# Stick-breaking sums over the keys in float32r, with the softplus split in two parts

## The chip, the cores and the metric

The kernel runs on one core of a Trainium2 chip. The metric is the device time of one execution in microseconds (us). The engines of the core are named as in the profile: PE (TensorE, matrix products), PEld (its weight loads), DVE (VectorE), ACT (ScalarE), POOL (GpSimd) and SP, whose queue starts the transfers of the weights.

## The reference, cut to what matters

The program is a stack of layers over 256 tokens of width 1024: feed-forward, gated linear attention, feed-forward, feed-forward, **stick-breaking attention**, feed-forward, and then a second block with a mixture of experts. Only the stick-breaking layer is changed:

```python
z = einsum('bhtd,bhsd->bhts', q_blk, k) * scale          # 16 heads of 64
mask = s_pos[None, :] < t_pos[:, None]
sp = where(mask, softplus(z), 0.0)
rem = cumsum(sp, axis=3, reverse=True) - sp              # over the keys s, backwards
weights = where(mask, exp(log_sigmoid(z) - rem), 0.0)
o = einsum('bhts,bhsd->bhtd', weights, v)
```

Since log_sigmoid(z) is z - softplus(z), the exponent is z minus the sum of softplus over this key and all later ones that the query may see.

## The kernel before

All matrix products of the layers before the experts are made in float32r, in three terms: an operand x is cut into a part `hi` that float32r holds (an ACT Copy) and the rest `lo` (a DVE subtraction), and hi*hi + lo*hi + hi*lo is summed (`mm3`, L449 to L451). Weights come in tiles of 128x2048 (`raw`), which ACT and DVE cut into `whi` (L253) and `wlo` (L256) up to three tiles ahead of their use (`feed.ahead`). Nothing reorders the program: each engine's instructions stand in the order in which the code writes them.

The stick-breaking layer is `sb`. It takes the 16 heads in four groups `g` of four. For each group it projects queries (`proj_t`, 48 matmuls into `pj`), keys (the same) and values (`proj_v`, 48 matmuls into `pv`, L608 to L610). The attention of a group runs in three steps that are laid between the projections of the next group: `scores` after the next queries, `weights` after the next keys, `heads_out` after the next values. For the last group there are no further projections: `scores` follows its own values, and the output projection (`out_proj`, tiles `acco`) gives the cover instead, 36 matmuls between `scores` and `weights`, and 36 between `weights` and `heads_out`.

Each step does two halves `hc` (two heads each), half 0 first on every engine. A half holds the logits transposed (keys on the partitions), 384 columns for each head: 256 queries against the first 128 keys, and the last 128 queries against the last 128 keys. For a half

- `scores` makes the logits in plain f32 on PE (L870, L873), adds the mask with bf16 products (L876, L877), and then softplus(z) = max(z,0) + log(1+exp(-|z|)): Abs, Exp and Ln on ACT (L879 to L881, 128x768 each) and one DVE instruction (L882), into the tile `e`;
- `weights` subtracts the sums over the keys on PE, in plain f32: `ntri` (a triangle of -1) within a block of 128 keys (L887, L889), and `nones` (all -1) for what the second block adds to the queries of the first (L888). The trace shows every plain f32 matmul as two instructions. Then ACT takes Exp into `w` (L891);
- `heads_out` multiplies with the values (L899, L900) and cuts the result into `ohi` and `olo`.

Of the kernel before, what the change touches and what calls it, by code (L numbers as in the profile page):

```python
# [8 lines left out]
F32 = mybir.dt.float32  # L9
F32R = mybir.dt.float32r  # L10
# [3 lines left out]
AF = mybir.ActivationFunctionType  # L14
# [3 lines left out]
P = 128  # L18
T = 256
# [275 lines left out]
def body(ctx, tc, xin, small, cst, masks, groups, wts, out):  # L295
    nc = tc.nc
# [7 lines left out]
    mm = nc.tensor.matmul  # L304
# [30 lines left out]
    def C(name, a=0, b=None):  # L335
        o, w = coff[name]
        return ct[:, o + a:o + (w if b is None else b)]
# [3 lines left out]
    ident = C("ident")  # L341

    def bank(name):
        return psum.tile([P, 512], F32, name=name, tag="ps", bufs=4)
# [3 lines left out]
    def banks(name):  # L348

        return half2["pool"].tile([P, 2, 512], F32, name=name, tag="two", bufs=2)  # L350
# [6 lines left out]
    def tables(name):  # L357
        if in_place[0] != name:
            nc.scalar.preload_act_table_set(name)
        in_place[0] = name  # L360
# [59 lines left out]
    def stats_sums(ms=None):  # L420
        if ms is None:
            ms = bank("ms")
        held["ms"] = ms
        for tb in range(2):
            mm(ms[:, tb:tb + 1], lhsT=ssq[:, 0, tb * P:tb * P + P], rhs=one, start=True, stop=True)
        rsqrt(base, ms[:, 0:2], 2, 1.0 / D, "rs", rt)
# [158 lines left out]
    def proj_t(key, post=None, mid=None, first=False, ahead=None):  # L585

        hi, lo = feed.take(key)
        b = bank("pj")
        for s, c, opens in order(first):
            o = c * 256 + s * P  # L590
            mm3(b[:, s * T:(s + 1) * T], hi[:, o:o + P], lo[:, o:o + P], hhi[:, c, :], hlo[:, c, :], opens, c == ND - 1)
            if mid is not None and s == 0 and c == ND - 1:
                mid()
        if post is not None:
            post(b)
        feed.ahead(ahead)
        return b

    def proj_v(key, evac, mid=None, post=None):

        hi, lo = feed.take(key)
        b = bank("pv")
        for tb in range(2):
            ts = slice(tb * P, tb * P + P)
            o = b[:, tb * T:(tb + 1) * T]
            for c in range(ND):
                w = slice(c * 256, c * 256 + 256)
                mm(o, lhsT=hhi[:, c, ts], rhs=hi[:, w], start=(c == 0), stop=False)  # L608
                mm(o, lhsT=hhi[:, c, ts], rhs=lo[:, w], start=False, stop=False)
                mm(o, lhsT=hlo[:, c, ts], rhs=hi[:, w], start=False, stop=(c == ND - 1))  # L610
            if mid is not None and tb == 0:
                mid()
        for tb in range(2):
            evac(tb, b[:, tb * T:(tb + 1) * T])
        if post is not None:
            post()
        feed.ahead()
# [231 lines left out]
    def sb(gnext):  # L849
        with tc.tile_pool(name="sb", bufs=2) as pool, tc.tile_pool(name="sba", bufs=1, space=PS) as pacc:  # L850
            half2["pool"] = pacc
            ohi = pool.tile([P, ND, T], F32R, name="ohi", bufs=1)
            olo = pool.tile([P, ND, T], F32R, name="olo", bufs=1)
            cb = pool.tile([P, 2, P], BF16, name="cb", bufs=1)
            nones = pool.tile([P, P], F32, name="nones", bufs=1)
            nc.gpsimd.tensor_copy(cb[:, 0, :], ident)
            nc.gpsimd.tensor_copy(cb[:, 1, :], C("negs"))
            nc.gpsimd.memset(nones, -1.0)
            ntri = C("ntri")
            rb2 = rb[:, None, :].to_broadcast([P, 2, T])  # L860
            W3 = 3 * P
            def pair(b):
                return b.rearrange("p (s t) -> p s t", s=2)

            def scores(hc, qg, kg):

                z = banks("z")
                for k in range(2):
                    ps = slice(64 * k, 64 * k + 64)
                    mm(z[:, k, :T], lhsT=kg[ps, hc, :P], rhs=qg[ps, hc, :], start=True, stop=False, skip_group_check=True)  # L870
                for k in range(2):
                    ps = slice(64 * k, 64 * k + 64)
                    mm(z[:, k, T:W3], lhsT=kg[ps, hc, P:], rhs=qg[ps, hc, P:], start=False, stop=False,  # L873
                       skip_group_check=True)
                for k in range(2):
                    mm(z[:, k, :P], lhsT=cb[:, 0, :], rhs=cb[:, 1, :], start=False, stop=False, skip_group_check=True)  # L876
                    mm(z[:, k, T:W3], lhsT=cb[:, 0, :], rhs=cb[:, 1, :], start=False, stop=False, skip_group_check=True)  # L877
                e = pool.tile([P, 2, W3], F32, name="e", bufs=2)
                nc.scalar.activation(e, z[:, :, :W3], AF.Abs)  # L879
                nc.scalar.activation(e, e, AF.Exp, scale=-1.0)  # L880
                nc.scalar.activation(e, e, AF.Ln, bias=1.0)  # L881
                nc.vector.scalar_tensor_tensor(e, z[:, :, :W3], 0.0, e, op0=OP.max, op1=OP.add)  # L882
                return z, e

            def weights(z, e):
                for k in range(2):
                    mm(z[:, k, :T], lhsT=ntri, rhs=e[:, k, :T], start=False, stop=False, skip_group_check=True)  # L887
                    mm(z[:, k, P:T], lhsT=nones, rhs=e[:, k, T:], start=False, stop=False, skip_group_check=True)  # L888
                    mm(z[:, k, T:W3], lhsT=ntri, rhs=e[:, k, T:], start=False, stop=True, skip_group_check=True)  # L889
                w = pool.tile([P, 2, W3], F32, name="w", bufs=2)  # L890
                nc.scalar.activation(w, z[:, :, :W3], AF.Exp)  # L891
                return w

            def heads_out(n, hc, w, vg):
                o = bank("o")
                for k in range(2):
                    ps = slice(64 * k, 64 * k + 64)
                    vs = slice((2 * hc + k) * 64, (2 * hc + k) * 64 + 64)
                    mm(o[ps, :T], lhsT=vg[:, 0, vs], rhs=w[:, k, :T], start=True, stop=False)  # L899
                    mm(o[ps, P:T], lhsT=vg[:, 1, vs], rhs=w[:, k, T:], start=False, stop=True)  # L900
                nc.scalar.activation(ohi[:, n, :], o[:, :T], AF.Copy)
                nc.vector.tensor_sub(olo[:, n, :], o[:, :T], ohi[:, n, :].bitcast(F32))

            def attention(g, qg, kg, vg):
                ze = [scores(hc, qg, kg) for hc in range(2)]
                yield
                ws = [weights(*x) for x in ze]
                yield
                for hc in range(2):
                    heads_out(2 * g + hc, hc, ws[hc], vg)  # L910
                yield

            steps = iter(())
            tables(EXPLN)
            for g in range(4):
                qg = pool.tile([P, 2, T], F32, name="qg")
                kg = pool.tile([P, 2, T], F32, name="kg")
                vg = pool.tile([P, 2, T], F32, name="vg")

                def q_out(b):  # L920
                    nc.vector.scalar_tensor_tensor(qg, pair(b), 0.125, rb2, op0=OP.mult, op1=OP.mult)

                bq = proj_t(("col", "sb_w_in", 0, g * 256), post=q_out if g else lambda b: stats_sums(), first=g == 0)
                next(steps, None)

                def k_out(b):
                    if not g:
                        q_out(bq)
                    nc.vector.tensor_mul(kg, pair(b), rb2)

                proj_t(("col", "sb_w_in", 0, 1024 + g * 256), post=k_out, mid=stats_spread if g == 0 else None)
                next(steps, None)
                proj_v(("col", "sb_w_in", 0, 2048 + g * 256), lambda tb, b: nc.scalar.activation(
                    vg[:, tb, :], b, AF.Copy, scale=rt[:, tb:tb + 1]))
                next(steps, None)
                steps = attention(g, qg, kg, vg)
            next(steps, None)
            out_proj("sb_w_out", lambda c: (ohi[:, c, :], olo[:, c, :]), gnext, early=list(range(6)), mid=steps)
# [694 lines left out]
    ffn("ffn2", 0, g_ffn1[:, 8:16])  # L1633
    ffn("ffn1", 1, g_mix[:, 8:16])
    sb(g_ffn2[:, 8:16])
    late = ctx.enter_context(tc.tile_pool(name="late", bufs=1))
    g12 = late.tile([P, ND], F32, name="g12")
# [58 lines left out]
```

## Time and profile before

| | |
|---|---|
| time, 3 runs | 1588.01, 1588.44, 1591.41 us; median 1588.44 |
| profiled execution | 1587.87 us, of which its span (first to last instruction) is 1585.5 us |
| PE busy in the span | 1431.3 us, 90% |
| DVE, ACT busy | 781.4 us (49%), 569.1 us (36%) |
| the chain that ended last | PE 68%, DMA 23%, DVE 5%, ACT 3% |
| where `sb` lies | its projections run from about 679 to 770 us, its output projection to about 800 us |

Busy shares are means over the whole span; the stage that is changed is some 8% of it. What counts there is which engine the others wait for, and that is read from the stage itself.

### The profile page before, as it was taken

The numbers are of one execution on the slowest core, as the hardware profiler recorded it, in microseconds if no ns is written. First come the engines' busy times: TensorE is split into PE (matmuls) and PEld (weight loads), VectorE is DVE, ScalarE is ACT, GpSimd is POOL, SyncE is SP. The second block draws the span as 40 slices with busy tenths as digits, with TensorE's granted clock in tenths as the row PEclk, the third lists the DMA queues.
The fourth block names the chain that finished last, engine by engine and source line by source line (L and its number), as shares of the span: only waits on it lengthen the run. The fifth ranks groups of instructions, "written<-read, shape, count | busy, mean of one in ns | idle before, by whom it ended". The sixth has DMA issues, their size and how long they took to land.

```text
span 1585.5 us, 31150 instructions
## 1 busy us (share of the span) xinstructions
PE 1431.3 (90%) x13785; PEld 1249.2 (79%) x13785; DVE 781.4 (49%) x1163; ACT 569.1 (36%) x708; POOL 52.8 (3%) x53
## 2 busy tenths in 40 slices
PE   8999999999999999999999999999996666676665
PEld 7999999999999999999999999989752233232222
DVE  6755677776667666673376556776320010010001
ACT  5444455454444544464554444444210000000000
POOL 0000014100000000000010000100000000000000
PEclk9999999999999999999999999999899888788887
DMA  7655544246554555443345555427899999999997
GB/s 291 236 189 187 186 144 166 98 171 229 200 184 159 224 192 213 185 161 127 114 160 213 187 187 186 162 81 318 342 420 420 421 421 419 421 421 420 421 420 286
DMA packets 56474, 395.60 MB, mean 250 GB/s; under 512 B 6400, under 2 KB 6656, under 8 KB 8976
## 3 DMA queue, kind: packets, MB, share of 16 engines
q1 hardware_dynamic: 56336, 393.57, 63.9%
q8 instruction: 110, 1.80, 0.4%
q14 instruction: 28, 0.23, 0.0%
HBM read 392.50 MB, written 1.05 MB: 248 GB/s over the span
## 4 chain that ended last, share of the span: by engine, by line
PE 68%; DMA 23%; DVE 5%; ACT 3%; issue 1%; SPq 0%; ACTq 0%
PE gu L451 10%; PE gu L449 10%; PE gu L450 10%; DMA raw<-wts 7%; DMA whi<-wts 6%; PE acc L451 5%; PE acc L449 5%; PE acc L450 5%; DMA sX<-wts 4%; PE pj L449 3%; DMA sF<-wts 3%; PE pj L450 3%; PE pj L451 3%; DMA h<-wts 2%; PE gx L1492 2%; DVE wlo L256 1%
## 5 line engine op out<-in xcount | busy, mean ns | idle before, releaser
L256 DVE TENSOR_TENSOR wlo<-raw,whi 128x2048 fp32r<-128x2048 f32 (+1 forms) x186 | 413.0, 2231 | 200.0 <-ACT whi L253 200.0
L449 PE MATMUL gu<-hhi,whi 128*128 128x256 f32 x1408 | 394.8, 280 | 7.3 <-ACT whi L253 7.3
L451 PE MATMUL gu<-hhi,wlo 128*128 128x256 f32 x1408 | 394.3, 280 | 1.5 <-DVE wlo L256 1.5
L450 PE MATMUL gu<-hlo,whi 128*128 128x256 f32 x1408 | 394.0, 280 | 0.0
L253 ACT ACTIVATE whi<-raw 128x2048 fp32r<-128x2048 f32 (+1 forms) x186 | 341.9, 1851 | 45.1 <-issue 34.8
L449 PEld LDWEIGHTS gu<-hhi,whi 128*128 128x128 f32 x1408 | 266.5, 189 | 7.3 <-ACT whi L253 7.3
L451 PEld LDWEIGHTS gu<-hhi,wlo 128*128 128x128 f32 x1408 | 267.5, 190 | 2.1 <-DVE wlo L256 2.1
L450 PEld LDWEIGHTS gu<-hlo,whi 128*128 128x128 f32 x1408 | 268.0, 190 | 0.2 <-DVE hlo L400 0.2
L449 PE MATMUL acc<-ahi,whi 128*128 128x256 f32 x704 | 196.0, 278 | 0.0
L450 PE MATMUL acc<-alo,whi 128*128 128x256 f32 x704 | 196.0, 278 | 0.0
L451 PE MATMUL acc<-ahi,wlo 128*128 128x256 f32 x704 | 196.0, 278 | 0.0
L1531 DVE TENSOR_SCALAR gp<-ptb,ct 128x256 f32<-128x256 f32 x32 | 15.5, 483 | 281.7 <-PE ptb L1529 281.7
L1498 ACT ACTIVATE gp<-gx 128x256 f32<-128x256 f32 x32 | 12.3, 383 | 393.7 <-PE gx L1492 393.7
L489 ACT ACTIVATE sg<-gp 128x256 f32<-128x256 f32 x88 | 36.8, 418 | 290.9 <-DVE gp L488 280.6
L450 PEld LDWEIGHTS acc<-alo,whi 128*128 128x128 f32 x704 | 132.9, 189 | 0.0
L451 PEld LDWEIGHTS acc<-ahi,wlo 128*128 128x128 f32 x704 | 132.8, 189 | 0.0
L449 PEld LDWEIGHTS acc<-ahi,whi 128*128 128x128 f32 x704 | 132.1, 188 | 0.0
L449 PE MATMUL pj<-hhi,whi 128*128 128x256 f32 x416 | 118.4, 285 | 0.0
L450 PE MATMUL pj<-hlo,whi 128*128 128x256 f32 x416 | 116.7, 280 | 0.7 <-DVE hlo L400 0.7
L451 PE MATMUL pj<-hhi,wlo 128*128 128x256 f32 x416 | 116.5, 280 | 0.0
L450 PEld LDWEIGHTS pj<-hlo,whi 128*128 128x128 f32 x416 | 79.3, 191 | 0.9 <-DVE hlo L400 0.9
L449 PEld LDWEIGHTS pj<-hhi,whi 128*128 128x128 f32 x416 | 79.1, 190 | 1.0 <-issue 1.0
(438 smaller groups left out, 2007.3 us busy)
## 6 DMA issues: line engine op xcount, KB each, us to landing
raw<-wts SPq DMA_DIRECT2D x218, 1024.0 KB, 4.9
whi<-wts SPq DMA_DIRECT2D x37, 1024.0 KB, 19.8
wlo<-wts SPq DMA_DIRECT2D x37, 1024.0 KB, 19.8
sX<-wts SPq DMA_DIRECT2D x10, 1024.0 KB, 19.8
sA<-wts SPq DMA_DIRECT2D x10, 1024.0 KB, 19.8
sF<-wts SPq DMA_DIRECT2D x10, 1024.0 KB, 19.8
sG<-wts SPq DMA_DIRECT2D x10, 1024.0 KB, 19.8
sC<-wts SPq DMA_DIRECT2D x10, 1024.0 KB, 19.8
```

The costliest lines, as they stand in the source:

```text
L253: self.nc.scalar.activation(hi[:, o], r[:, o], AF.Copy)
L256: self.nc.vector.tensor_sub(lo[:, o], r[:, o], hi[:, o].bitcast(F32))
L449: mm(o, lhsT=whi, rhs=xhi, start=start, stop=False, skip_group_check=True)
L450: mm(o, lhsT=whi, rhs=xlo, start=False, stop=False, skip_group_check=True)
L451: mm(o, lhsT=wlo, rhs=xhi, start=False, stop=stop, skip_group_check=True)
L489: nc.scalar.activation(sg, gp, AF.Silu)
L1492: mm(b[rows[q], :W], lhsT=x[:, c, e % 8, :], rhs=w[:, o:o + W], start=(c == 0), stop=(c == ND - 1), skip_group_check=True)
L1498: nc.scalar.activation(s, b[:, :W], AF.Copy)
L1531: V.tensor_scalar(pt, b[:, :T], C("slot"), None, op0=OP.is_equal)
```

## The change

The sums over the keys are made in float32r. For this the softplus is split as the weights are: after DVE's L882 (now L889) ACT copies `e` into a float32r tile `hi` (L890), and DVE subtracts to get `lo` (L891). `weights` then makes four products for each head in place of three: `ntri` times 384 columns of `hi`, the same of `lo`, `nones` times 256 columns of `hi`, the same of `lo`. So that one product of 384 columns can take the place of two, the logits are laid out with the second key block first, and so that the `nones` product is 256 columns wide, `hi` and `lo` have 128 columns of zeros ahead of the data, which are written once at the start of `sb`. `ntri` and `nones` become float32r tiles that ACT writes, also at the start (L859, L860, L864). The two mask products of 128 columns become one of 256.

```diff
--- before.py
+++ after.py
@@ -852,11 +852,16 @@
             ohi = pool.tile([P, ND, T], F32R, name="ohi", bufs=1)
             olo = pool.tile([P, ND, T], F32R, name="olo", bufs=1)
             cb = pool.tile([P, 2, P], BF16, name="cb", bufs=1)
-            nones = pool.tile([P, P], F32, name="nones", bufs=1)
+            nones = pool.tile([P, P], F32R, name="nones", bufs=1)
+            ntri = pool.tile([P, P], F32R, name="ntri", bufs=1)
             nc.gpsimd.tensor_copy(cb[:, 0, :], ident)
             nc.gpsimd.tensor_copy(cb[:, 1, :], C("negs"))
-            nc.gpsimd.memset(nones, -1.0)
-            ntri = C("ntri")
+            nc.scalar.activation(ntri, C("ntri"), AF.Copy)
+            nc.scalar.activation(nones, ident, AF.Copy, scale=0.0, bias=-1.0)
+            es = [[pool.tile([P, 2, 512], F32R, name=f"e{n}{i}", bufs=1) for n in ("hi", "lo")] for i in range(2)]
+            for x in es:
+                for y in x:
+                    nc.scalar.activation(y[:, :, :P], cb, AF.Copy, scale=0.0)
             rb2 = rb[:, None, :].to_broadcast([P, 2, T])
             W3 = 3 * P
             def pair(b):
@@ -864,29 +869,34 @@
 
             def scores(hc, qg, kg):
 
+
                 z = banks("z")
                 for k in range(2):
                     ps = slice(64 * k, 64 * k + 64)
-                    mm(z[:, k, :T], lhsT=kg[ps, hc, :P], rhs=qg[ps, hc, :], start=True, stop=False, skip_group_check=True)
+                    mm(z[:, k, P:W3], lhsT=kg[ps, hc, :P], rhs=qg[ps, hc, :], start=True, stop=False, skip_group_check=True)
                 for k in range(2):
                     ps = slice(64 * k, 64 * k + 64)
-                    mm(z[:, k, T:W3], lhsT=kg[ps, hc, P:], rhs=qg[ps, hc, P:], start=False, stop=False,
+                    mm(z[:, k, :P], lhsT=kg[ps, hc, P:], rhs=qg[ps, hc, P:], start=False, stop=False,
                        skip_group_check=True)
                 for k in range(2):
-                    mm(z[:, k, :P], lhsT=cb[:, 0, :], rhs=cb[:, 1, :], start=False, stop=False, skip_group_check=True)
-                    mm(z[:, k, T:W3], lhsT=cb[:, 0, :], rhs=cb[:, 1, :], start=False, stop=False, skip_group_check=True)
+                    mm(z[:, k, :T], lhsT=cb[:, 0, :], rhs=cb[:, 1:2, :].to_broadcast([P, 2, P]), start=False, stop=False,
+                       skip_group_check=True)
                 e = pool.tile([P, 2, W3], F32, name="e", bufs=2)
+                hi, lo = (x[:, :, P:] for x in es[hc])
                 nc.scalar.activation(e, z[:, :, :W3], AF.Abs)
                 nc.scalar.activation(e, e, AF.Exp, scale=-1.0)
                 nc.scalar.activation(e, e, AF.Ln, bias=1.0)
                 nc.vector.scalar_tensor_tensor(e, z[:, :, :W3], 0.0, e, op0=OP.max, op1=OP.add)
-                return z, e
+                nc.scalar.activation(hi, e, AF.Copy)
+                nc.vector.tensor_sub(lo, e, hi.bitcast(F32))
+                return z, es[hc]
 
             def weights(z, e):
                 for k in range(2):
-                    mm(z[:, k, :T], lhsT=ntri, rhs=e[:, k, :T], start=False, stop=False, skip_group_check=True)
-                    mm(z[:, k, P:T], lhsT=nones, rhs=e[:, k, T:], start=False, stop=False, skip_group_check=True)
-                    mm(z[:, k, T:W3], lhsT=ntri, rhs=e[:, k, T:], start=False, stop=True, skip_group_check=True)
+                    for i, x in enumerate(e):
+                        mm(z[:, k, :W3], lhsT=ntri, rhs=x[:, k, P:], start=False, stop=False, skip_group_check=True)
+                    for i, x in enumerate(e):
+                        mm(z[:, k, P:W3], lhsT=nones, rhs=x[:, k, :T], start=False, stop=(i == 1), skip_group_check=True)
                 w = pool.tile([P, 2, W3], F32, name="w", bufs=2)
                 nc.scalar.activation(w, z[:, :, :W3], AF.Exp)
                 return w
@@ -896,8 +906,8 @@
                 for k in range(2):
                     ps = slice(64 * k, 64 * k + 64)
                     vs = slice((2 * hc + k) * 64, (2 * hc + k) * 64 + 64)
-                    mm(o[ps, :T], lhsT=vg[:, 0, vs], rhs=w[:, k, :T], start=True, stop=False)
-                    mm(o[ps, P:T], lhsT=vg[:, 1, vs], rhs=w[:, k, T:], start=False, stop=True)
+                    mm(o[ps, :T], lhsT=vg[:, 0, vs], rhs=w[:, k, P:], start=True, stop=False)
+                    mm(o[ps, P:T], lhsT=vg[:, 1, vs], rhs=w[:, k, :P], start=False, stop=True)
                 nc.scalar.activation(ohi[:, n, :], o[:, :T], AF.Copy)
                 nc.vector.tensor_sub(olo[:, n, :], o[:, :T], ohi[:, n, :].bitcast(F32))
```

On ACT, in a group's `scores`, the order of work was this (`e` is the softplus tile, `z` the logits; the last row is the cut of a weight tile that follows):

```order
L879 ACTIVATE e<-z 128x768
L880 ACTIVATE e<-e 128x768
L881 ACTIVATE e<-e 128x768
L879 ACTIVATE e<-z 128x768
L880 ACTIVATE e<-e 128x768
L881 ACTIVATE e<-e 128x768
L253 ACTIVATE whi<-raw 128x2048
```

and on ACT it is now this (`ehi_7725` and `ehi_7727` are the `hi` tiles of half 0 and half 1):

```order
L886 ACTIVATE e<-z 128x768
L887 ACTIVATE e<-e 128x768
L888 ACTIVATE e<-e 128x768
L890 ACTIVATE ehi_7725<-e 128x2x384
L886 ACTIVATE e<-z 128x768
L887 ACTIVATE e<-e 128x768
L888 ACTIVATE e<-e 128x768
L890 ACTIVATE ehi_7727<-e 128x2x384
L253 ACTIVATE whi<-raw 128x2048
```

The copy of half 0, which reads what DVE's L889 writes, stands ahead of the Abs of half 1.

On PE, in `weights`, a half was this:

```order
L887 MATMUL z<-e,ct 128x256
L888 MATMUL z<-e,nones 128x128
L889 MATMUL z<-e,ct 128x128
L887 MATMUL z<-e,ct 128x256
L888 MATMUL z<-e,nones 128x128
L889 MATMUL z<-e,ct 128x128
```

and half 1 on PE is now this (`elo_7728` is its `lo` tile; each of these is one instruction):

```order
L897 MATMUL z<-ehi_7727,ntri 128x384
L897 MATMUL z<-elo_7728,ntri 128x384
L899 MATMUL z<-ehi_7727,nones 128x256
L899 MATMUL z<-elo_7728,nones 128x256
L897 MATMUL z<-ehi_7727,ntri 128x384
L897 MATMUL z<-elo_7728,ntri 128x384
L899 MATMUL z<-ehi_7727,nones 128x256
L899 MATMUL z<-elo_7728,nones 128x256
```

The product that needs `lo` is the second of eight, so six follow it.

On ACT, at the start of `sb`, six instructions come in ahead of the table load and of the cuts of three weight tiles:

```order
 L399 ACTIVATE hhi<-xT,sm 128x256 x2
 L409 ACTIVATE ssq<-xT 128x512
+L859 ACTIVATE ntri<-ct 128x128
+L860 ACTIVATE nones<-ct 128x128
+L864 ACTIVATE ehi_7725<-cb 128x2x128
+L864 ACTIVATE elo_7726<-cb 128x2x128
+L864 ACTIVATE ehi_7727<-cb 128x2x128
+L864 ACTIVATE elo_7728<-cb 128x2x128
 L359 ACT_TABLE_LOAD
 L253 ACTIVATE whi<-raw 128x2048 x3
```

Everything behind them on ACT, up to the first group's values, moves back by what the six take.

## Rows read from the trace of the kernel before

**Rows 1.** Stretch of the stage: its length, then each engine busy us

```profile
697.00:721.00 24.00, 24.00 (x205) 22.96 (x204) 9.98 (x7) 13.35 (x15) 0.00 (x0) 1.00 0.49 180
```

**Rows 2.** PE in order of time: start, us; second and last of 48

```profile
705.51 0.28 PE L450 MATMUL pj<-hlo,whi 128*128 128x256 f32 x1
...
710.93 0.28 PE L451 MATMUL pj<-hhi,wlo 128*128 128x256 f32 x1
```

**Rows 3.** The chain that ended last, first group's `weights`: start us, us, what

```profile
711.21 0.43 PE z L887 x2
711.64 0.22 PE z L888 x2
711.86 0.22 PE z L889 x2
...
714.72 0.12 PE pv L608
```

**Rows 4.** ACT in order of time, first group

```profile
704.35 0.81 ACT L879 ACTIVATE e<-z 128x768 f32<-128x768 f32 x1 [2.39 <-PE z L877]
...
706.08 0.84 ACT L881 ACTIVATE e<-e 128x768 f32<-128x768 f32 x1
706.83 0.79 ACT L879 ACTIVATE e<-z 128x768 f32<-128x768 f32 x1
...
709.28 1.90 ACT L253 ACTIVATE whi<-raw 128x2048 fp32r<-128x2048 f32 x1
```

**Rows 5.** DVE in order of time, first group

```profile
706.96 0.96 DVE L882 SCALAR_TENSOR_TENSOR e<-z,e 128x768 f32<-128x768 f32 x1 [0.89 <-ACT e L881]
709.41 0.96 DVE L882 SCALAR_TENSOR_TENSOR e<-z,e 128x768 f32<-128x768 f32 x1 [1.50 <-ACT e L881]
```

**Rows 6.** ACT by line and form: count, busy us, mean ns, idle before

```profile
L836 ACT ACTIVATE ohi<-kT 128x512 fp32r<-128x512 f32 x2 | 1.3, 632 | 2.1 <-DVE kT L835 2.1
...
L253 ACT ACTIVATE whi<-raw 128x2048 fp32r<-128x2048 f32 x178 | 337.0, 1906 | 43.9 <-issue 34.8 <-PE pj L450 3.3 <-DVE rst L380 2.1
...
L901 ACT ACTIVATE ohi<-o 128x256 fp32r<-128x256 f32 x8 | 2.7, 386 | 4.4 <-PE o L900 4.4
```

**Rows 7.** DVE by line and form, same columns

```profile
L842 DVE TENSOR_TENSOR olo<-kT,ohi 128x512 fp32r<-128x512 f32 x2 | 1.4, 686 | 0.1
...
L256 DVE TENSOR_TENSOR wlo<-raw,whi 128x2048 fp32r<-128x2048 f32 x178 | 406.1, 2292 | 197.3 <-ACT whi L253 197.3
```

**Rows 8.** DVE in order of time, last group

```profile
774.87 0.96 DVE L882 SCALAR_TENSOR_TENSOR e<-z,e 128x768 f32<-128x768 f32 x1
```

**Rows 9.** The chain that ended last, last group's `weights`

```profile
777.32 0.43 PE z L887 x2
...
780.84 0.12 PE acco L449
```

**Rows 10.** Stretches at two thin spells of PE; PEclk after the busy times

```profile
290.00:291.00 1.00, 1.00 (x11) 1.00 (x11) 0.28 (x2) 0.00 (x0) 0.00 (x0) 1.00 0.00 0
808.00:810.00 2.00, 1.45 (x8) 1.45 (x9) 1.76 (x10) 2.00 (x2) 0.00 (x0) 0.76 0.16 25
810.00:812.00 2.00, 2.00 (x12) 2.00 (x11) 1.86 (x6) 0.14 (x1) 0.00 (x0) 0.50 0.88 369
812.00:814.00 2.00, 2.00 (x17) 2.00 (x17) 2.00 (x2) 0.00 (x0) 0.00 (x0) 0.88 0.31 131
```

**Rows 11.** PE in order of time: the instructions at the two thin spells

```profile
288.97 1.84 PE L806 MATMUL oss<-ones,w 128*128 128x1 f32 x16
...
808.55 0.38 PE L451 MATMUL gu<-hhi,wlo 128*128 128x256 f32 x1 [1.25 <-DVE wlo L256]
```

**Rows 12.** ACT in order of time, start of `sb`

```profile
685.28 5.53 ACT L253 ACTIVATE whi<-raw 128x2048 fp32r<-128x2048 f32 x3
```

**Rows 13.** DVE in order of time, start of `sb`

```profile
688.21 4.50 DVE L256 TENSOR_TENSOR wlo<-raw,whi 128x2048 fp32r<-128x2048 f32 x2
```

**Rows 14.** PE in order of time, first use of a `wlo` in `proj_v`

```profile
691.99 0.28 PE L609 MATMUL pv<-wlo,hhi 128*128 128x256 f32 x1
```

## The prediction

> **What bounds the kernel now.** I read the busy times of the stage first, then the chain that ended last, then the engines in order of time. In a stretch that holds one whole group, PE is busy for all 24.00 us at full clock, DVE for 9.98, ACT for 13.35 [rows 1]: PE sets the pace here, and the others have time to spare. The chain agrees: it runs along PE through `weights`, from the first `ntri` product at 711.21 to the first value product at 714.72, with nothing between [rows 3]. So a product taken from PE shortens the stage, but only while what `weights` reads is ready before PE comes to it. That is the second thing to read. DVE finishes the softplus of half 1 at 709.41 + 0.96 = 710.37 [rows 5], and the last product of the keys' projection starts at 710.93 [rows 2]. The spare time in front of `weights` is then about 0.6 us. The reader is to see this number beside what the change puts into that gap.
>
> **What is removed: plain f32 products.** In the chain one head takes 0.43 + 0.22 + 0.22 = 0.87 us, and the four heads of a group 714.72 - 711.21 = 3.51 us [rows 3]. A float32r product of 256 columns takes (710.93 - 705.51) / 46 = 0.118 us in a stream of them [rows 2]. No row shows one of 384 columns. It cannot be cheaper than 0.118 us, and at the plain f32 pace, 0.43 us for two instructions of 256 columns [rows 3], it would be 0.33 us. I take the column's share of the float32r stream, 0.177 us, since that is the same type and operation. A head is then 2 x 0.177 + 2 x 0.118 = 0.59 us, a half 1.18, a group 2.36: 1.15 us less than 3.51, and 4.6 us in all, if nothing is waited for. The mask has as many columns as before in fewer products, and I count nothing for it; PE streams there, and two products fewer can only save some hundredths for each half.
>
> **What is added: a copy and a subtraction in series.** Between the softplus and the products stand now an ACT Copy and a DVE subtraction of 768 columns. Between the rows of 512 and 2048 columns, ACT's Copy is 632 + 256 x (1906 - 632) / 1536 = 844 ns [rows 6] and DVE's subtraction 686 + 256 x (2292 - 686) / 1536 = 954 ns [rows 7]. The nearest rows from below are 632 and 686 ns, which is the lower end; nothing near speaks for much more than the line between the rows.
>
> The Trainium skill ("ScalarE: Activation LUTs", Rules for kernel authors) budgets about 0.3 us for an ACTIVATE and 0.83 ns for each element, an estimate of 0.94 us here. The rows give 0.84 and are taken. By that estimate from the Trainium skill each of two copies in a group's series would be 0.1 us longer, and the time 0.8 us more.
>
> What decides is the order on ACT. Half 0's Copy waits for DVE, and half 1's Abs stands behind it. Before, half 1's Abs began at 706.83, before DVE had even begun half 0's last step at 706.96 [rows 4, 5]. Step by step for the first group, with 0.04 us from the end of one engine's work to the start of the next (706.92 to 706.96, [rows 4, 5]):
>
> - DVE ends half 0 at 706.96 + 0.96 = 707.92. ACT copies from 707.96 to 708.80.
> - Half 1's Abs starts 0.09 before that ends (706.83 against 706.92, [rows 4]), at 708.71, in place of 706.83.
> - DVE's last softplus step comes 709.41 - 706.83 = 2.58 after the Abs [rows 4, 5]: 711.29 to 712.25.
> - Copy of half 1: 712.29 to 713.13. Subtraction: 713.17 to 714.12.
>
> PE has half 0 in time (its `lo` is there at 708.84 + 0.95 = 709.79), does it from 711.21 to 712.39, makes one product when `hi` of half 1 comes, and waits for `lo` until 714.16. Behind it stand seven products: 0.177 + 2 x 0.118 + 0.59 = 1.00 us. The first product after a wait took 0.38 us where the stream shows 0.28 [rows 2, 11], 0.10 us to refill. The group ends at 714.16 + 0.10 + 1.00 = 715.26, not 714.72: **0.54 us later**, although its products are shorter. The second and third group repeat the first: 1.62 us.
>
> In the last group the cover is 36 products of the output projection instead of 48, and DVE's softplus of half 0 starts late, at 774.87 [rows 8]. The same steps: half 0 ends at 775.83, copy to 776.71, half 1's Abs at 776.62, DVE 779.20 to 780.16, copy to 781.04, subtraction to 782.03. PE wants to start at 777.32 [rows 9], waits for half 0's `lo` (777.70), is through with it at 778.84 and then waits until 782.07. It ends at 783.17 in place of 780.84 [rows 9]: **2.33 us later**. Together 3.95 us.
>
> Behind the delayed instructions ACT has a cut of a weight tile (at 709.28, [rows 4]) and DVE the evacuation of the keys and the same cut. They come some 4 us later, but are for a tile three projections on, and the keys are read a projection later; ACT and DVE are busy only about half of the stretch [rows 1]. I count nothing, and without that cover each 0.1 us would be 0.1 us of PE.
>
> **The clock.** The wait has a second price. After a wait of 1.25 us in a thin spell [rows 11] the granted clock fell from 2.4 GHz to 1.2: means of 0.76, 0.50 and 0.88 over three stretches of 2 us are 0.96 + 2.00 + 0.48 = 3.44 us at half clock [rows 10], which costs half of that, 1.72 us. But 1.84 us of products of one column left it at 1.00 [rows 10, 11]. In the last group PE has 782.07 - 778.84 = 3.2 us with one product in it, longer than both: I take one fall there, since dense work follows. In the first three it is 714.16 - 712.39 = 1.8 us with one product, like the spell that did no harm: I take none, but not with confidence.
>
> [...]
>
> **The start of `sb`.** Six ACT instructions come ahead of three cuts. None is larger than 128x256, which takes 386 ns [rows 6]: from nothing to 2.3 us. The first cut then starts at 685.28 + 2.3 = 687.6 at the latest and takes 5.53 / 3 = 1.84 [rows 12], and DVE's part of it, 4.50 / 2 = 2.25 [rows 13], ends at 691.7. PE first needs it at 691.99 [rows 14]. It is hidden, by 0.3 us; beyond that each 0.1 us late is 0.1 us lost.
>
> **The sum.** 1.62 + 2.33 + 1.72 = 5.67 us on the profiled execution's 1587.87 (its span of 1585.5 and 2.4 around it): 1593.5 us. That execution is 0.6 us below the median of the runs shown, 1588.44, and within their spread. What follows `sb` starts when PE and DVE hand it on and so moves as a whole; I know of nothing there that takes the delay back.
>
> **The rivals.**
>
> - *The clock holds.* Stalls as above, no fall: 1587.87 + 3.95 = 1591.8. For it: the one-column spell. Against: three microseconds with one product.
> - *The clock falls in the first groups too*: one to three more falls of 1.72, 1595.2 to 1598.7. For it: the fall after only 1.25 us of waiting. Against: 1.84 us of one-column products without one. [...]
> - *The split is cheaper*: at 632 and 686 ns, each group's series is 2 x 0.21 + 0.27 = 0.69 us shorter. The first three groups then gain 0.15 each, the last loses 1.64: 1.2 us more, 1589.1, or 1590.8 with the fall.
> - *Faster: half 1 does not wait for half 0's copy.* If ACT went on to half 1's Abs, `lo` of half 1 would be there about 1.8 us earlier (708.71 back to 706.83), PE would not stall in the first three groups, and up to the whole 4.6 us would be kept: 1583.3. It decides from 3.95 / 4 = 1.0 us less in each group's series. For it: ACT and DVE have the time [rows 1]. Against: the order on ACT, which the rows show kept.
> - *The 384 columns run at another price*: three such products stand behind `lo` in each group, so from 4 x 3 x (0.118 - 0.177) = -0.7 us to 4 x 3 x (0.33 - 0.177) = +1.8 us. This only widens the others.
>
> **How the numbers follow.** Stall with one fall 0.50 (1593.5; by itself 1592.5 to 1595), clock holds 0.17, more falls 0.15, cheaper split 0.12, faster 0.06. About 0.2%, 3.2 us, is what a measurement of this kernel can tell from no change, so slower begins at 1591.6, which cuts the second case in half. Slower: 0.50 + 0.15 + 0.09 = 0.74; same: 0.08 + 0.12 = 0.20; faster 0.06. The range from 1589.5 to 1597.5 leaves out the faster case, the lowest of the cheap split and three further falls, some 0.15.
>
> **What would show it.** In the profile after: L890 of about 0.84 us and L891 of 0.95; half 1's Abs some 1.9 us later against half 0's than before; waits of PE in `weights` for half 1, some 0.8 us for `hi` (ACT) and as much again for `lo` (DVE) in each of the first three groups, over 2 us and 0.8 in the last; float32r products of 384 columns at 0.17 to 0.18 us; one stretch of half clock behind the last group. I would be wrong if PE does not wait for `lo` there, if the split takes 0.7 us or less, or if the first value projection waits for its `wlo`.

## The result and the profile after

| | before | after |
|---|---|---|
| median of the runs, measured beside each other | 1584.95 us (20 runs) | 1592.65 us (20 runs) |
| ratio, 95% interval | | 1.0054, 1.0039 to 1.0070 |
| profiled execution | 1587.87 us | 1594.99 us |

The changed kernel is slower by 7.7 us between the medians, and by about 8.6 us (6.2 to 11.1) by the ratio, which leaves out one slow run of after (1615.52 us). The forecast was 5.1 us over the median then known, 1588.44. More runs put the kernel before at 1584.95, 3.5 us lower, so that 1593.5 lies nearer to 1592.65 than the forecast of the change lay to the change.

One execution differs from the next by several us, and much of that lies outside `sb`: its first Abs comes at 704.35 before the change and at 698.09 behind it. So I compare a piece of the trace that holds all of the change but its start: from the first Abs of `sb` (ACT) to the first addition of its output projection into `xT` (DVE, L441). The start lies ahead of the piece. There, from the last L409 on ACT to the first Abs, it is 704.35 - 683.36 = 20.99 us before and 698.09 - 677.11 = 20.98 after. Behind the piece, from that addition to the product that the next layer waits for (L451 of `gu`, 808.55 before [rows 11], 811.50 after), it is 16.10 us in both: nothing there takes the delay back. Before the change, the piece runs from 704.35 [rows 4] to 792.45, 88.10 us. DVE in order of time, kernel before:

```profile
792.45 0.69 DVE L441 TENSOR_TENSOR xT<-xT,acco 128x512 f32<-128x512 f32 x1 [5.14 <-PE acco L451]
```

After, ACT in order of time, both halves of the first group, the columns as in [rows 4]:

```profile
698.09 0.81 ACT L886 ACTIVATE e<-z 128x768 f32<-128x768 f32 x1 [2.38 <-PE z L882]
698.93 0.85 ACT L887 ACTIVATE e<-e 128x768 f32<-128x768 f32 x1
699.81 0.85 ACT L888 ACTIVATE e<-e 128x768 f32<-128x768 f32 x1
701.68 0.85 ACT L890 ACTIVATE ehi<-e 128x768 fp32r<-128x768 f32 x1 [1.02 <-DVE e L889]
702.44 0.80 ACT L886 ACTIVATE e<-z 128x768 f32<-128x768 f32 x1
...
706.01 0.84 ACT L890 ACTIVATE ehi<-e 128x768 fp32r<-128x768 f32 x1 [1.02 <-DVE e L889]
706.76 1.89 ACT L253 ACTIVATE whi<-raw 128x2048 fp32r<-128x2048 f32 x1
```

and DVE of the same execution, the two steps of half 1 and the end of the piece:

```profile
705.02 0.96 DVE L889 SCALAR_TENSOR_TENSOR e<-z,e 128x768 f32<-128x768 f32 x1 [1.50 <-ACT e L888]
706.89 0.96 DVE L891 TENSOR_TENSOR elo<-e,ehi 128x768 fp32r<-128x768 f32 x1 [0.91 <-ACT ehi L890]
...
795.40 0.69 DVE L441 TENSOR_TENSOR xT<-xT,acco 128x512 f32<-128x512 f32 x1 [5.15 <-PE acco L451]
```

The piece is 795.40 - 698.09 = 97.31 us, 9.21 longer. The reader is to see the 1.02 us in brackets on ACT: it waits for DVE with half 0's Copy, and half 1's Abs, which needs neither, starts 702.44 - 698.09 = 4.35 us behind half 0's, where it was 2.48 [rows 4]. What comes of it on PE, first group, in order of time:

```profile
704.53 0.34 PE L897 MATMUL z<-ehi,ntri 128*128 128x384 f32 x1
704.71 0.34 PE L897 MATMUL z<-elo,ntri 128*128 128x384 f32 x1
704.88 0.28 PE L899 MATMUL z<-ehi,nones 128*128 128x256 f32 x1
...
705.59 0.28 PE L899 MATMUL z<-elo,nones 128*128 128x256 f32 x1
706.91 0.44 PE L897 MATMUL z<-ehi,ntri 128*128 128x384 f32 x1 [1.04 <-ACT ehi L890]
707.90 0.44 PE L897 MATMUL z<-elo,ntri 128*128 128x384 f32 x1 [0.55 <-DVE elo L891]
...
709.01 0.28 PE L608 MATMUL pv<-whi,hhi 128*128 128x256 f32 x1
```

Half 0 runs at the short products' pace, and half 1 waits twice. All waits of PE in the stage, by engine and line waited for, total us, times, longest:

```profile
PE z L897 <- ACT ehi L890: 5.2, 4, 2.1
PE z L897 <- DVE elo L891: 2.7, 5, 0.6
```

Before, PE waited for nothing in `weights`. And the granted clock, in stretches of 2 us behind the waits of the four groups (columns as in [rows 1], PE alone: length, busy, PEclk):

```profile
706.00:708.00 2.00, 0.54 (x2) 1.00 0.00 0
708.00:710.00 2.00, 2.00 (x13) 0.80 0.00 0
710.00:712.00 2.00, 2.00 (x11) 0.50 0.18 25
712.00:714.00 2.00, 2.00 (x17) 0.85 0.83 266
732.00:734.00 2.00, 0.93 (x5) 1.00 0.00 0
734.00:736.00 2.00, 1.46 (x10) 1.00 0.00 0
...
760.00:762.00 2.00, 2.00 (x12) 0.60 0.03 8
...
782.00:784.00 2.00, 2.00 (x10) 0.50 0.03 8
```

It falls to half in three groups of four: the first, the third and the last. The second has the same waits and keeps 1.00. With the forecast's own terms, 3.95 of waits and three times 1.72, the sum is 9.11 us; 9.21 was measured. So near a match is partly luck: experiment 11 will put the waits at 4.63 and three falls at 4.58.

### The profile page after: what moved, and what is told of

Its sections match the earlier page's. It is cut to its first block, busy times and chain, and to the rows that moved or that the text cites. A ratio compares the mean times of both kernels' runs of the same rounds, so it can differ in the third digit from the quotient of the medians.

```text
span 1593.2 us, 31061 instructions
## 1 busy us (share of the span) xinstructions
PE 1434.2 (90%) x13737; PEld 1251.3 (79%) x13737; DVE 789.9 (50%) x1171; ACT 577.1 (36%) x722; POOL 52.7 (3%) x52
## 4 chain that ended last, share of the span: by engine, by line
PE 64%; DMA 25%; DVE 5%; ACT 5%; issue 1%; POOL 0%; SPq 0%; ACTq 0%
DMA wlo<-wts 10%; PE gu L451 9%; PE gu L450 9%; PE gu L449 9%; DMA raw<-wts 5%; DMA xT<-wts 5%; DMA sC<-wts 5%; PE acc L450 5%; PE acc L451 5%; PE acc L449 5%; PE pj L449 3%; PE pj L450 2%; PE pj L451 2%; PE pv L608 1%; DVE wlo L256 1%; PE pv L609 1%
## 5 line engine op out<-in xcount | busy, mean ns | idle before, releaser
L451 PE MATMUL gu<-hhi,wlo 128*128 128x256 f32 x1408 | 392.9, 279 | 1.5 <-DVE wlo L256 1.4
L451 PEld LDWEIGHTS gu<-hhi,wlo 128*128 128x128 f32 x1408 | 266.3, 189 | 2.5 <-DVE wlo L256 2.4
L451 PE MATMUL acc<-ahi,wlo 128*128 128x256 f32 x704 | 195.2, 277 | 0.0
L451 PEld LDWEIGHTS acc<-ahi,wlo 128*128 128x128 f32 x704 | 132.2, 188 | 0.0
L451 PE MATMUL pj<-hhi,wlo 128*128 128x256 f32 x416 | 118.1, 284 | 0.0
```

The source lines that it names most:

```text
L451: mm(o, lhsT=wlo, rhs=xhi, start=False, stop=stop, skip_group_check=True)
```

## The experiments

The theory: half 0's Copy holds up half 1 on ACT, PE waits, and some waits cost a fall of the clock too. Rivals: the split is too long wherever it stands; the layout or the start of `sb` costs; the clock costs nothing. Each kernel ran in five rounds beside the kernel before. The table gives, for the profiled execution of each, the time from a group's first Abs to the next group's (the last group: to L441), the sum of the four, and the ratio of the times of all runs to those of before.

| kernel | groups, us | sum | ratio, 95% interval |
|---|---|---|---|
| before | 24.40, 24.39, 19.11, 20.20 | 88.10 | |
| after | 26.63, 25.11, 21.37, 24.20 | 97.31 | 1.0054, 1.0039 to 1.0070 |
| 1 after again | 24.89, 26.83, 19.82, 25.41 | 96.95 | 1.0076, 1.0050 to 1.0102 |
| 2 order on ACT | 23.19, 23.41, 18.12, 21.19 | 85.91 | 1.0001, 0.9977 to 1.0026 |
| 3 filled waits | 25.10, 25.11, 19.83, 23.71 | 93.75 | 1.0027, 1.0003 to 1.0050 |
| 4 start only | 24.40, 24.39, 19.11, 20.21 | 88.11 | 1.0008, 0.9986 to 1.0030 |
| 5 layout only | 24.34, 24.33, 18.86, 20.28 | 87.81 | 0.9993, 0.9971 to 1.0015 |
| 6 DVE's copy | 23.00, 22.99, 17.71, 20.71 | 84.41 | 0.9984, 0.9961 to 1.0007 |
| 7 order, last group mixed | 23.39, 23.39, 18.12, 19.87 | 84.77 | 0.9968, 0.9948 to 0.9988 |
| 8 order on ACT again | 23.39, 23.40, 18.12, 22.69 | 87.60 | 0.9954, 0.9931 to 0.9977 |
| 9 DVE's copy, last group mixed | 22.78, 22.77, 17.72, 20.00 | 83.27 | 0.9974, 0.9955 to 0.9993 |
| 10 as 7 again | 23.39, 23.40, 18.11, 19.88 | 84.78 | 0.9970, 0.9942 to 0.9998 |
| 11 filled waits, shorter | 25.10, 25.11, 19.83, 22.69 | 92.73 | 1.0044, 1.0019 to 1.0068 |

**1. The changed kernel again.** No edit.

> The changed kernel once more, beside the next three on one chip. Theory (half 1's softplus waits on ACT behind half 0's copy, PE then waits for `hi` and `lo` of half 1, and the granted clock falls behind some of these waits): the stretch from the first Abs of `sb` to the first addition of its output projection is again about 97 us (88.1 before, 97.3 after), 4.0 us of it from waits net of the shorter products and 1.7 us for each fall, with two to four falls; in all 7 to 10 us slower than before. Rival (the falls are chance): the waits stay at 4.0 us and the falls differ from one execution to the next, so that the stretch comes out anywhere between 92 and 99 us.

The sum is 96.95, with two falls: in the second group (26.83, where it took 25.11 without one in the first trace) and in the last, there for much longer. Stretches of PE with PEclk:

```profile
738.00:740.00 2.00, 0.68 (x3) 1.00 0.00 0
740.00:742.00 2.00, 1.72 (x10) 0.80 0.00 0
742.00:744.00 2.00, 2.00 (x11) 0.50 0.00 0
...
784.00:786.00 2.00, 0.07 (x1) 0.89 0.00 0
786.00:788.00 2.00, 1.69 (x5) 0.50 0.03 8
788.00:790.00 2.00, 2.00 (x11) 0.50 0.00 0
790.00:792.00 2.00, 2.00 (x11) 0.50 0.45 82
792.00:794.00 2.00, 2.00 (x18) 0.90 0.97 410
```

So both held in part: the waits are there every time and are about as long (7.4 us in all, 7.9 in the first trace), while which group loses the clock changes from one execution to the next.

**2 and 8. The order on ACT.** Both halves' splits stand behind half 1's logarithm:

```diff
-                hi, lo = (x[:, :, P:] for x in es[hc])
...
+                return z, es[hc], e
+
+            def split(z, x, e):
+                hi, lo = (y[:, :, P:] for y in x)
                 nc.scalar.activation(hi, e, AF.Copy)
                 nc.vector.tensor_sub(lo, e, hi.bitcast(F32))
-                return z, es[hc]
+                return z, x
...
-                ze = [scores(hc, qg, kg) for hc in range(2)]
+                ze = [split(*x) for x in [scores(hc, qg, kg) for hc in range(2)]]
```

> Same operations, but the copies and subtractions of both halves stand behind the logarithm of half 1 on ACT, so that half 1's Abs waits for nothing. Theory (the order on ACT makes the wait): half 1's Abs starts 2.5 us behind half 0's as before the change, `lo` of half 1 is there about 7.9 us behind the first Abs, PE waits for next to nothing in the first three groups, which end some 1.0 us earlier than in the kernel before; the last group ends some 0.7 us later; no fall of the clock in the first three groups. In all 2 us faster than before, about 10 us faster than the changed kernel. Rival (the split's own work is too long for the cover, whatever its order): PE still waits for `lo` of both halves, and the time stays within 3 us of the changed kernel.

> The second experiment once more, for more runs: whether its shorter stretch, 85.9 us against 88.1, reaches the whole time. Theory: 2 us or 0.14% faster than the kernel before, ratio 0.9986. Rival (what follows `sb` takes it back): ratio 1.000 or above.

ACT in order of time, first group of experiment 2:

```profile
708.18 0.85 ACT L887 ACTIVATE e<-e 128x768 f32<-128x768 f32 x1
708.93 0.79 ACT L885 ACTIVATE e<-z 128x768 f32<-128x768 f32 x1
...
711.39 0.83 ACT L893 ACTIVATE ehi<-e 128x768 fp32r<-128x768 f32 x1
712.51 0.85 ACT L893 ACTIVATE ehi<-e 128x768 fp32r<-128x768 f32 x1 [0.29 <-DVE e L888]
```

Half 1's Abs is back at 2.47 us behind half 0's (706.46), the same operations take the same time, and the first three groups become 1.21, 0.98 and 0.99 us shorter than before the change. The order was the cause; the rival falls. In the last group PE now waits for half 0, and the group is 0.99 longer:

```profile
777.01 0.44 PE L900 MATMUL z<-ehi,ntri 128*128 128x384 f32 x1 [0.97 <-ACT ehi L893]
778.13 0.44 PE L900 MATMUL z<-elo,ntri 128*128 128x384 f32 x1 [0.68 <-DVE elo L894]
```

In experiment 8 that same wait brought a fall, 22.69 against 21.19, and with it the gain of the sum shrank from 2.19 to 0.50 us. Over whole times the same program measured 1.0001 and 0.9954. These two sets of 12 runs lie 0.47% apart, over 7 us, far more than the layer's gain of 0.03 to 0.14%; so the whole times can't show it, and the groups must.

**3 and 11. Products in the waits.** Ahead of half 1's products, and between its first `hi` and `lo` product, 12 products into columns that nothing reads (ahead of it 36 in the last group of experiment 3; the edit shown is that of 11):

```diff
-            def weights(z, e):
+            def fill(z, n):
+                for _ in range(n):
+                    mm(z[:, 1, W3:], lhsT=cb[:, 0, :], rhs=cb[:, 1, :], start=False, stop=False, skip_group_check=True)
+
+            def weights(z, e, n=0):
+                fill(z, n)
...
+                        if n and k == 0 and i == 1:
+                            fill(z, 12)
...
-                ws = [weights(*x) for x in ze]
+                ws = [weights(*x, n=(0, 12)[i]) for i, x in enumerate(ze)]
```

> The changed kernel with products that add nothing anyone reads (bf16, 128 columns, into unused columns of half 1's bank): 12 ahead of half 1's products, 36 in the last group, and 12 between its `hi` and its `lo` products. They keep PE busy while it waits. Theory (1.7 us for each fall of the clock, the rest waiting): the granted clock stays at 1.00 through the groups, the waits' 4 us stay, the stretch is 92 to 93.5 us, and the time is 3 to 5 us less than that of the changed kernel, 4 to 5 us over the kernel before. Rival (all of it is waiting, the clock costs nothing): the time stays that of the changed kernel or grows by what the additional products delay.

> The third experiment with 12 additional products in the last group too, in place of 36, which had made the group's products themselves late by 1.2 us. Theory (waits 4 us, each fall 1.7 us): no fall, groups of 25.1, 25.1, 19.8 and 22.5 us, the stretch 92.3 to 92.8 us, 4.2 to 4.7 us over the kernel before and 4.5 us under the changed one. Rival (a wait of 1.2 us that nothing fills in the last group is enough for a fall): the last group is at 24.2 us and the stretch at 94.2.

Experiment 11, PE in order of time in the first group:

```profile
715.15 0.83 PE L896 MATMUL z<-cb 128*128 128x128 bf16 x12 [0.16 <-DVE e L889]
716.03 0.45 PE L904 MATMUL z<-ehi,ntri 128*128 128x384 f32 x1
716.32 0.85 PE L896 MATMUL z<-cb 128*128 128x128 bf16 x12
717.03 0.44 PE L904 MATMUL z<-elo,ntri 128*128 128x384 f32 x1
```

The wait is as long (half 1's first `hi` product comes 716.03 - 707.21 = 8.82 us behind the first Abs, and 706.91 - 698.09 = 8.82 in the trace of after), PE fills it, and PEclk is 1.00 in every stretch of all four groups, in both experiments. What is left is waiting: 92.73 - 88.10 = 4.63 us. What the fill took away is the clock's part: 97.31 - 92.73 = 4.58 us in the first trace of after, 96.95 - 92.73 = 4.22 in the second. In experiment 3 the 36 products ran from 782.37 for 2.17 us, past the end of half 1's Copy (782.35 + 0.84), and so made the last group itself about 1 us later (23.71 against 22.69): my edit's fault, mended in 11. The whole times (1.0027 and 1.0044) lie below those of after (1.0054 and 1.0076), but the intervals overlap; the groups decide here.

**4. The start alone.** The kernel before with the six ACT instructions at the start of `sb`:

```diff
+            ntri_r = pool.tile([P, P], F32R, name="ntri_r", bufs=1)
+            nones_r = pool.tile([P, P], F32R, name="nones_r", bufs=1)
+            nc.scalar.activation(ntri_r, C("ntri"), AF.Copy)
+            nc.scalar.activation(nones_r, ident, AF.Copy, scale=0.0, bias=-1.0)
+            es = [[pool.tile([P, 2, 512], F32R, name=f"e{n}{i}", bufs=1) for n in ("hi", "lo")] for i in range(2)]
+            for x in es:
+                for y in x:
+                    nc.scalar.activation(y[:, :, :P], cb, AF.Copy, scale=0.0)
```

> The kernel before, with only the six ACT instructions and the tiles that the change puts at the start of `sb`; products and softplus are those of before. Theory (hidden behind the projections ahead): the stretch is 88 us, no new wait of PE in the first value projection, the time that of the kernel before within 0.2%. Rival (the start costs, by late cuts or by where the tiles lie in memory): 1 us slower or more.

88.11 us against 88.10, and PE waits for nothing new. The piece begins behind the start, so the stretch ahead of it counts here: from the last L409 to the first Abs it is 704.63 - 683.65 = 20.98 us, against 20.99. The start is hidden.

**5. The layout alone.** The changed kernel with plain products from `e`:

```diff
-                nc.scalar.activation(hi, e, AF.Copy)
-                nc.vector.tensor_sub(lo, e, hi.bitcast(F32))
-                return z, es[hc]
+                return z, e
...
+                    mm(z[:, k, :T], lhsT=ntri.bitcast(F32), rhs=e[:, k, :T], start=False, stop=False, skip_group_check=True)
+                    mm(z[:, k, T:W3], lhsT=ntri.bitcast(F32), rhs=e[:, k, T:], start=False, stop=False, skip_group_check=True)
+                    mm(z[:, k, T:W3], lhsT=nones.bitcast(F32), rhs=e[:, k, :P], start=False, stop=True, skip_group_check=True)
```

> The changed kernel's layout, its one mask product for two, and its start of `sb`, but no split: the sums are again three plain f32 products for each head, taken from `e`. Theory (layout and mask products are worth nothing that can be measured, all of the change lies in the split): each group takes what it takes in the kernel before, 24.4 us from one group's first Abs to the next one's, the stretch from the first Abs of `sb` to the first addition of its output projection is 88.0 to 88.2 us, and no wait of PE in `weights`. Rival (the layout has a price of its own): the stretch is 0.5 us longer or more.

87.81, 0.29 less than before, not nothing: 0.06 in each of the first two groups, where one mask product stands for two, 0.25 in the third, and the last 0.08 longer. The third is no more than two executions of one program can differ by in a group: experiments 2 and 8 have 23.19 and 23.39 in the first. No price of the layout.

**6. DVE's copy.**

```diff
-                nc.scalar.activation(hi, e, AF.Copy)
+                nc.vector.tensor_copy(hi, e)
```

> The changed kernel with `hi` copied by DVE in place of ACT, so that ACT waits for nothing between the halves although the split stands in the same place of the program. Theory (it is half 1's Abs behind the waiting Copy on ACT that costs): half 1's Abs is 2.5 us behind half 0's again, PE hardly waits in the first three groups, each 1.0 to 1.2 us shorter than before the change; the last is 0.2 to 1.1 us longer, by the price of DVE's copy, which no row shows; stretch 84.8 to 86.2 us, no fall of the clock in the first three groups. Rival (any split placed between the halves makes half 1 late): the stretch stays above 92 us.

DVE in order of time, first group:

```profile
708.02 0.96 DVE L889 SCALAR_TENSOR_TENSOR e<-z,e 128x768 f32<-128x768 f32 x1 [0.89 <-ACT e L888]
709.01 0.56 DVE L890 CAST ehi<-e 128x768 fp32r<-128x768 f32 x1
709.60 0.96 DVE L891 TENSOR_TENSOR elo<-e,ehi 128x768 fp32r<-128x768 f32 x1
710.48 0.96 DVE L889 SCALAR_TENSOR_TENSOR e<-z,e 128x768 f32<-128x768 f32 x1
```

The split stands where the change put it, yet DVE hands from one step to the next without waiting for ACT between them, half 1's Abs is 2.48 us behind half 0's (707.89, 705.41), and PE's waits for `hi` and `lo` in the whole stage are 0.9 us. The sum is 84.41, 3.69 less than before the change, a little better than expected: the copy takes 0.56 us on DVE, where ACT's takes 0.84. The Trainium skill (VectorE: DVE Perf Modes, The perf-mode tier table) has a float32 copy at twice the rate of a float32 `tensor_tensor`; the trace agrees nearly, with 0.56 beside 0.96 us, a little over half. The first groups are 1.40 shorter, not 1.15. In the trace the products from the first of `weights` to the first value product take 714.23 - 711.86 = 2.37 us, as forecast; the mask gives 0.06, and where the remaining 0.2 comes from I have not tested. It is of the size of the scatter: experiment 9, the same in its first three groups, has 22.78, 22.77 and 17.72 there for the 23.00, 22.99 and 17.71 of this one.

**7, 9 and 10. The last group mixed.** There half 0 is split by DVE's copy and half 1 multiplied in plain f32 from `e` with the three products of experiment 5. In 7 and 10 the first three groups are those of experiment 2, in 9 those of experiment 6. Their core in 9:

```diff
-                nc.scalar.activation(hi, e, AF.Copy)
+                if plain:
+                    return z, e
+                nc.vector.tensor_copy(hi, e)
...
-                ze = [scores(hc, qg, kg) for hc in range(2)]
+                ze = [scores(hc, qg, kg, plain=g == 3 and hc == 1) for hc in range(2)]
```

> What the runs so far point to: in the first three groups both halves' split behind half 1's logarithm, as in the second experiment; in the last, where the cover is short, half 0 split with DVE's copy and half 1 left to plain f32 products from `e`. Theory: the first three groups 1.0 to 1.2 us shorter each, the last 0.0 to 0.4 us shorter than before the change, the stretch 84.2 to 85.0 us, in all some 3.5 us or 0.2% faster than the kernel before. Rival (the gain in the stretch is given back behind it): the stretch is as short, and the time that of the kernel before.

> DVE's copy, of 0.56 us in the sixth experiment, in all groups, and half 1 of the last group left to plain f32 products, as in the seventh. Theory: the groups add as they stood in those two runs, 23.00 + 22.99 + 17.71 + 19.87 = 83.6 us, 4.5 us less than before the change; the time is 0.2 to 0.4% less than that of the kernel before. Rival (the two do not add: the last group's plain products wait for DVE behind its longer queue): the last group is back at 20.2 us or more, and the stretch at 84 us or above.

> The seventh experiment once more, beside the ninth on one chip, for more runs. Theory: a stretch of 84.8 us, and a ratio near 0.997 to the kernel before, some 1 us behind the ninth. Rival (the 0.32% of the first time was scatter): ratio 0.999 or above.

Experiment 9, PE in order of time, last group, half 1 following half 0 with no wait:

```profile
768.50 0.44 PE L904 MATMUL z<-elo,ntri 128*128 128x384 f32 x1 [0.18 <-DVE elo L893]
...
769.48 0.28 PE L906 MATMUL z<-elo,nones 128*128 128x256 f32 x1
769.60 0.59 PE L899 MATMUL z<-e,ntri 128*128 128x256 f32 x2
```

All three have sums 3.3 to 4.8 us below the kernel before, and times 0.26 to 0.32% below it, with intervals that exclude 1. Both versions beat both kernels. Between them the sums put 9 ahead by 1.5 us; the times do not tell them apart.

## Why the prediction was right or wrong

- **The products' price: right.** A float32r product of 384 columns stands 0.18 us apart from the next (704.53, 704.71, 704.88), as taken; a group without waits 2.37 us, forecast 2.36.
- **The split's price: right.** Copy 0.845 against 0.844 us, subtraction 0.958 against 0.954. The rival of a cheaper split falls, and so does the longer Copy of 0.94 us that was estimated beside it.
- **The order on ACT and its wait: right.** From the first Abs, half 1's Abs comes at 4.35 us (forecast 708.71 - 704.35 = 4.36), its `lo` is there at 706.89 + 0.96 - 698.09 = 9.76 (9.77), the first value product comes at 709.01 - 698.09 = 10.92 (10.91). The wait is 1.04 + 0.55 us instead of twice 0.8: the division was off, the sum right. The rival that half 1 would not wait falls by these rows, and is what experiments 2 and 6 build.
- **The sum of the waits: nearly right.** 4.63 us in experiment 11, forecast 3.95. The groups without a fall are 0.5 to 0.7 longer (forecast 0.54), the last 2.49 (2.33).
- **The start of `sb`: right.** Its six instructions take 1.7 us (up to 2.3 was allowed); the first value product waits for nothing, and experiment 4 shows no cost.
- **The clock: wrong in number.** The failed step is "In the first three it is 1.8 us with one product, like the spell that did no harm: I take none, but not with confidence". In two traces of the changed kernel the clock fell after 3 of 6 such waits: in the first and third group of one, in the second of the other. In the last group, where a fall was forecast, it fell both times, once for twice as long. All falls together cost 4.6 and 4.2 us, where one of 1.72 was taken. So the likeliest case, "stall with one fall", is not what these traces show; the named rival "the clock falls in the first groups too" is, and it had 0.15. The row I leaned on, 1.84 us of one-column products [rows 11], was a spell in which PE had work all along, [rows 10]; here PE was busy for 0.54 of 2 us. The better guide was the wait of 1.25 us with a fall [rows 11], and it calls for a chance to each group in place of all or none: the same wait in front of the same product stands behind `sb` in all 13 traces, 1.25 or 1.26 us long, and the clock fell there in 7 of them (before, after, experiments 1, 3, 5, 10 and 11) and held in 6. Experiment 2, PE and its stretches, where it held:

```profile
808.48 0.38 PE L451 MATMUL gu<-hhi,wlo 128*128 128x256 f32 x1 [1.25 <-DVE wlo L256]
808.00:810.00 2.00, 1.52 (x13) 1.00 0.28 37
810.00:812.00 2.00, 2.00 (x20) 1.00 0.86 360
```

- The forecast's absolute time came out well by luck: its base was 3.5 us high, the clock's term 2.5 to 2.9 us low and the waits 0.7 low. Its base of 1587.87 also lay just below the three runs then known (1588.01 the lowest), not within their spread as it says.

Runs of the same program with a fall in different places, in `sb` and behind it, show that the waits of the program alone do not decide it. What else does is open. The Trainium skill (TensorE: Matmul & The Clock Gate, HAM oscillation) tells of a kernel in which each wait of some 3 to 5 us for a transfer, between bursts of products, put the clock back to half. The traces here show falls after shorter waits too, of 1 to 2 us, but only after some of them.

## What to carry to other kernels

Where two independent chains share an engine whose instructions run in the order written, put a step that waits for another engine behind the other chain's steps that don't, or on the engine that it would wait for: here that turned 9 us lost into 0.5 to 3.7 us won with the same products. Cheaper products shorten a stage only by as much as their operands are early; count that spare time (0.6 us here) before the products. A wait of a us or two in front of dense products should be priced twice, once for itself and once, with a chance, for the clock behind it.

## What the runs showed of the hardware

- The granted clock fell or held after one and the same wait: experiments 2 and 8, one program, with waits of 0.97 and 0.68 us (0.96 and 0.69 in 8) in the last group. It held in the first (no fall in 21.19 us) and fell in the second. Stretches of experiment 8:

```profile
768.00:770.00 2.00, 1.03 (x7) 1.00 0.95 401
770.00:772.00 2.00, 1.31 (x6) 0.74 0.00 0
772.00:774.00 2.00, 2.00 (x10) 0.50 0.04 8
774.00:776.00 2.00, 2.00 (x17) 0.91 0.24 33
```

- Time at half clock was not of one length: about 3.4 us for most falls (0.80 + 2.00 + 0.60 in the first group of after), and in the last group of experiment 1 some 6.8 (0.44 + 6.00 + 0.40), dense products running all through the second half of it.
- Products of no use kept the clock up: in 8 of 8 groups of experiments 3 and 11 there was no fall, in the last group of each with 1.2 us of wait left unfilled; without them it fell in 5 of 8 groups.
- A table load on ACT took 1.28 us after the change, and the next cut started with its end: 679.37 + 1.28 = 680.65, 680.66.
